# Spatial gating's columns in a two-layer hybrid backbone: features as the stationary operand, then a turn by chunk

## The chip, the cores and the metric

One core of one Trainium2 chip runs the whole program. The metric is device microseconds for one execution, taken as the median of several runs.

## The reference

Two layers over 512 latent tokens and 256 context tokens, 1024 features each. A layer is a half-step SwiGLU network, a token mixing, and another half-step SwiGLU network, each ahead of a normalisation that two conditions modulate. The token mixing projects its normalised input h once:

```
px = hx @ w_in[l]                     # 1024 -> 512 q, 512 k, 512 v, 512 u, 512 vs, 2048 gates
o_a = neighbourhood_attention(q, k, v, ...)
o_b = chunk_spatial_gating(gelu(u), gelu(vs), ln_g, ln_b, w_s, b_s)

def chunk_spatial_gating(u, v, ln_g, ln_b, w_s, b_s):
    vn = layernorm(v, ln_g, ln_b)     # over the 512 features of a token
    s = einsum('gpq,bnqgc->bnpgc', w_s, vn as chunks of 128 tokens, 4 groups of 128 features) + b_s
    return u * s
```

The context passes through the whole mixing in layer 0; in layer 1, the last, it only gives keys and values. Everything is float32 in and out.

## The kernel before

Features lie on partitions, tokens along the free axis. h is 16 tiles of 128 features by 768 tokens (512 latent, then 256 context): eight hold the high part and eight the low part of a float32 number split in two (hh, hl). A weight unit is 128 x 1024 numbers (512 KB); SyncE loads it (line 233), ScalarE writes its high part (line 222) and GpSimd the low part (line 223). A product is then three matmuls: high by high, high by low, low by high.

There are two forms of product. In `block` (line 327, with `mm3`, line 315) the weights are stationary, 128 columns of them, and h moves: 512 latent columns and, in layer 0, 256 context columns. The result has features on partitions. In `by_token` (line 942) 128 tokens of h are stationary and 256 columns of weights move, so that the result has tokens on partitions. `values` (line 954) uses it, as the attention needs its values by token, and so does `vs_half` (line 1184), since the layer norm of the gating reduces over features and its mixing over the 128 tokens of a chunk.

The latent tokens are ordered by grid column with the eight rows innermost. A gating chunk of 128 tokens is therefore every fourth latent column: `tokens(n)` (line 1179) gives `t[:, n:NX:4]` for the four latent chunks, and 128 neighbouring columns for the two of the context, which only layer 0 has (`n_ch` is 6 in layer 0 and 4 in layer 1). `vs_half(half)` makes 256 of the 512 features for all chunks, two chunks to a PSUM bank, and ScalarE copies each bank into tiles `vs` (line 1198).

The order of work on every engine is the order in which the program emits it. A list of tasks is run one after the other (`run`, line 300); each yields now and then, and at each yield `step` (line 288) runs one piece of the head of each of three lists, `side2` (rotary embedding) first, then `side` (attention, and behind it `gating`), then `side3`. So a piece of attention (scores, weighted sum, transposes of the shares, in `attention`, line 1096) stands between pieces of the products on TensorE. `by_token` is emitted whole, one yield a chunk; `block` yields every `EVERY[l]` row blocks (2 in layer 0, 3 in layer 1), and its callers once more at the end. PSUM has eight banks, from one list; the tiles of 128 x 768 come from one list of 38 (`t3`).

The tasks of a mixing run in this order: k and q of heads 0 to 3, `values(0)`, q and k of heads 4 to 7, `vs_half(0)`, `values(1)`, four `u_block` (line 1164: a `block` whose banks ScalarE copies into a tile, line 1172), `vs_half(1)`, then `gating` is put behind the attention, then sixteen blocks of gates (line 1285), and the merge. `gating` (line 1229) takes the gelu of the vs tiles (line 1236), normalises them by chunk and multiplies by the chunk's mixing weights; GpSimd multiplies the result into u (line 1227), again with a step of four for latent chunks.

Of the kernel before, what the change touches and what calls it, by code (L numbers as in the profile page):

```python
# [13 lines left out]
P = 128  # L14
# [52 lines left out]
# ---------------------------------------------------------------- host layout  # L67
# [27 lines left out]
def bias_layout(rpb):  # L95
    """Per head and kind of query tile, rpb laid out over (query, key); masked keys hold MASKED."""
# [17 lines left out]
def cols_units(w, order=None):  # L114
    """[K, N] -> [N/128, 128, (K/128) * 128]: one unit for each block of 128 columns."""
    k, n = w.shape
    return w.reshape(k // P, P, n // P, P).transpose(2, 1, 0, 3).reshape(n // P, P, k)


def close_units(w):  # L120
    """[K, 1024] -> [K/128, 128, 1024]: blocks of 128 by 128, all rows of the first columns first, eight to a unit."""
    n = w.shape[0] // P
    return w.reshape(n, P, KD, P).transpose(2, 0, 1, 3).reshape(n, KD, P, P).transpose(0, 2, 1, 3).reshape(n, P, D)


def half_units(w):
    """[1024, 512] -> [2 column halves, 2 k halves, 128, 4 * 256]."""
    return w.reshape(2, 4, P, 2, 256).transpose(3, 0, 2, 1, 4).reshape(4, P, 1024)


def layout(inp):
# [9 lines left out]
    # for each 128 columns of both of the first two: [128, 8 chunks of rows, 2 * 128 columns]  # L141
# [9 lines left out]
    for l in range(DEPTH):  # L151
        for n in ("1", "2"):
# [9 lines left out]
            q, k, half_units(w[:, 1024:1536]), cols_units(w[:, 1536:2048]), half_units(w[:, 2048:2560]),  # L162
# [26 lines left out]
# ---------------------------------------------------------------- weights  # L189
# [8 lines left out]
class Stream:  # L198
    """Loads weight units ahead of their use and splits each into two float32r parts."""

    def __init__(self, nc, pool, units, n_raw, n_hi):
        self.nc, self.pool, self.units = nc, pool, units
        # one slot spare: a load does not wait for the readers emitted last
# [4 lines left out]
    def advance(self, most=1):  # L208
        """Emit loads while there is room, and the splits of at most so many units."""
# [46 lines left out]
# ---------------------------------------------------------------- device  # L256
class Core:
# [12 lines left out]
    # ---- tiles  # L270
# [9 lines left out]
    # ---- scheduling of the emission  # L280
    def task(self, units, gen, own=False):
        """own: the task itself takes and drops its units."""
# [32 lines left out]
    # ---- products  # L315
    def mm3(self, out, groups, w, xs, first, last):
        """out[g] += w.T @ x over one block of 128 rows, in three float32r products."""
# [9 lines left out]
    def block(self, out, groups, unit, ks, xs, every=4):  # L327
        """One 128-column block: ks = columns of the unit for each k, xs = (hi, lo) for each k."""
# [7 lines left out]
    # ---- setup  # L336
    def setup(self):
# [12 lines left out]
        # brings in the table of the first norm's root ahead of it  # L350
        nc.scalar.activation(out=self.sm(16, "nw")[:, :1], in_=self.ones[:, :1], func=AF.Sqrt)
        # the two conditions sixteen times over, for each k
# [24 lines left out]
    # ---- tables of the token mixing and, in their place, the conditions for the modulation  # L377
# [20 lines left out]
    # ---- modulation  # L398
    def ada_units(self, l, idx):
        """Steps of one unit each, which together make mods[l][:, idx]."""  # L400
# [3 lines left out]
        def part(d, unit):  # L404
            """128 columns of the modulation, on partitions: sums over the rows for both conditions."""
# [34 lines left out]
    def extras(self, n):  # L440
        """On average n of the modulations' steps."""
# [6 lines left out]
    def require(self, l, idx):  # L448
        """The modulations up to this one, whatever of them is left."""
# [13 lines left out]
    # ---- norms  # L463
# [14 lines left out]
    def rowsum(self, box, grp):  # L478
        """Tiles of squares summed over partitions, four side by side, each on 32 partitions."""
# [11 lines left out]
    def rstd(self, box, grp, waits=(1, 1, 1), keep=False):  # L491
        """1 / sqrt(mean + eps) of the squares, on every partition (in PSUM, or in SBUF)."""
# [36 lines left out]
    def norm(self, l, i, box, h, grp, waits=(1, 1, 1), keep=False):  # L529
        """h[:, grp] = rmsnorm(x) * g * (1 + scale) + shift, in two float32r parts."""  # L530
# [31 lines left out]
    def split(self, name, src, grps):  # L562
        """(hi, lo) of a float32 tile or of its column groups."""
# [10 lines left out]
    # ---- accumulate into the residual stream  # L574
# [7 lines left out]
    def close(self, l, idx, units, xs, groups, box, after):  # L582
        """The last rows of a product into the stream, group after group; the norm of the first group
        runs beside the products of the second."""
        ks = len(xs)

        def gen():
            left = list(units)
            # brings in the table of the norm's root ahead of it
# [25 lines left out]
    # ---- first products of a phase, group after group  # L615
    def opening(self, blocks, groups, h, done):
        """Blocks of one unit each, the norm of each group (one of two in the background) just ahead of
        its products; done gets the PSUM tiles of each block."""
        def gen():
            out = [{} for _ in blocks]  # L620
            left = list(blocks)
            for gi, grp in enumerate(groups):
                self.drain_to(1 - gi)
                for o in out:
                    # two halves share their bank
# [21 lines left out]
    # ---- FFN  # L647
    def ffn(self, l, f, groups, hbox, xgroups, box, after, start=False):
# [38 lines left out]
        def begin():  # L687
            """The first modulation by columns, so that the products begin with its first columns."""
# [4 lines left out]
            def load(d):  # L693
                """Columns of the first two modulations, three chunks of rows to a tile."""
# [122 lines left out]
    # ---- the end  # L817
    def finish(self, groups, box):
        """The last norm; the products of the first of two groups fill the waits of the second."""
# [4 lines left out]
        def slot(d, grp):  # L824
            """Where the chunk goes: up to three chunks leave together."""
# [45 lines left out]
    # ---- token mixing  # L871
    def mixing(self, l, hbox, hgroups, xgroups, box, after):
# [14 lines left out]
        # q and k: rotary embedding on (even, odd) tiles of four heads  # L887
# [54 lines left out]
        def by_token(us, c, ps, at):  # L942
            """ps[:, at:at + 256] = h[:, tokens].T @ w, c = columns of h for the tokens."""
# [10 lines left out]
        def values(g):  # L954
            us = [unit(8 + 2 * g + s) for s in range(2)]

            def gen():
                # for each chunk and head (hi, lo) of 64 columns, six pairs to a tile
# [17 lines left out]
        # attention  # L976
# [12 lines left out]
        def stacks(raw):  # L989
            """One step for q, one for k."""  # L990
# [439 lines left out]
```

## Time and profile before

| | |
|---|---|
| median of three runs | 3034.73 us (3034.19 to 3035.49) |
| profiled execution, span from first to last instruction | 3031.9 us |
| between that span and the median | 2.8 us |
| TensorE busy in the span | 2998.1 us |
| VectorE, ScalarE, GpSimd busy | 1324.4, 906.4, 1138.1 us |
| mean DMA rate | 103 GB/s |

The page gives no total of its own for the profiled execution, so its time is its span and the 2.8 us that the median has beyond it. In the rows below, PE is TensorE's matmuls and PEld its weight loads, which overlap them; DVE is VectorE, ACT is ScalarE, POOL is GpSimd, SP is SyncE. "L950" is line 950 of the kernel. Names such as `ps<-whi,hh` give what is written and what is read. Matmuls are pipelined: a piece's length on the chain, or the distance from one start to the next, is what it costs the engine, while a matmul's own duration includes its way through the array. The chain of work that ended last is followed back from the last instruction; its pieces in order of time give the start, the length and the number of instructions.

### The profile page before, as it was taken

To read this page: it belongs to the slowest core of one execution; us is meant where nothing else is said; L and a number is where in the kernel's file an instruction comes from. 1 tells how busy PE (TensorE), PEld (TensorE's weight loads), DVE (VectorE), ACT (ScalarE), POOL (GpSimd) and SP (SyncE) were. 2 spreads that over 40 slices of the span, in tenths; PEclk is the share of its full clock that TensorE was granted. 3 is DMA by queue.
4 is the path that set the end of the run, shared out by engine and by line. 5 is a ranking of instruction groups with operands and counts; after the bars stand their busy time and mean duration, and the time that the engine had idled before them with its cause. 6 is when DMAs were issued, how large, how long until landed. Compare 5 with 4: busy or idle time off the path is not lost.

```text
span 3031.9 us, 41959 instructions
## 1 busy us (share of the span) xinstructions
PE 2998.1 (99%) x17036; PEld 2614.0 (86%) x17036; DVE 1324.4 (44%) x2256; ACT 906.4 (30%) x1493; POOL 1138.1 (38%) x708
## 2 busy tenths in 40 slices
PE   8999999999999999999999999999999999999998
PEld 5888888899998888888888888888888998888887
DVE  4554445536642444434445544544344643421113
ACT  4212112334652233111122411121233553332222
POOL 1323333444434243223233333332335545544443
PEclk9999999999999999999999999999999999999999
DMA  6333333333311132323333133332224322323222
GB/s 232 124 115 116 116 114 112 104 126 89 89 53 63 51 124 86 109 85 111 105 106 107 68 111 110 118 105 104 81 81 153 102 80 88 121 75 102 96 103 70
DMA packets 99888, 311.20 MB, mean 103 GB/s; under 512 B 12656, under 2 KB 14960, under 8 KB 99696
## 3 DMA queue, kind: packets, MB, share of 16 engines
q1 hardware_dynamic: 96704, 296.79, 29.2%
q0 software_dynamic: 2560, 11.54, 1.0%
q8 instruction: 134, 2.20, 0.3%
q14 instruction: 58, 0.48, 0.0%
q10 hardware_dynamic: 432, 0.20, 0.0%
HBM read 288.56 MB, written 8.39 MB: 98 GB/s over the span
## 4 chain that ended last, share of the span: by engine, by line
PE 95%; DVE 3%; DMA 1%; ACT 1%; issue 0%; POOL 0%; SPq 0%; ACTq 0%; DVEq 0%; POOLq 0%
PE ps L322 28%; PE ps L325 28%; PE ps L323 28%; PE ps L950 6%; PE ov L1073 1%; PE pt L1051 1%; DVE hl L550 1%; DVE nu L541 1%; PE sc L1016 0%; PE sc L1018 0%; DVE x L577 0%; PE ss L485 0%; DVE gt L1223 0%; DMA wraw<-up 0%; PE rs L519 0%
## 5 line engine op out<-in xcount | busy, mean ns | idle before, releaser
L223 POOL TENSOR_TENSOR wlo<-wraw,whi 128x1024 fp32r<-128x1024 f32 (+2 forms) x426 | 936.9, 2201 | 1606.1 <-ACT whi L222 1581.9
L322 PE MATMUL ps<-hh,whi 128*128 128x512 f32 (+1 forms) x3200 | 1115.1, 348 | 5.3 <-ACT hh L545 5.3
L323 PE MATMUL ps<-hl,whi 128*128 128x512 f32 (+1 forms) x3200 | 1049.0, 345 | 0.6 <-DVE hl L550 0.6
L325 PE MATMUL ps<-hh,wlo 128*128 128x512 f32 (+1 forms) x3200 | 906.5, 346 | 0.2 <-POOL wlo L223 0.2
L322 PEld LDWEIGHTS ps<-hh,whi 128*128 128x128 f32 x3200 | 602.2, 188 | 143.0 <-ACT hh L545 6.5
L222 ACT CAST whi<-wraw 128x1024 fp32r<-128x1024 f32 (+2 forms) x426 | 395.6, 931 | 997.4 <-PE ps L323 404.2
L323 PEld LDWEIGHTS ps<-hl,whi 128*128 128x128 f32 x3200 | 602.5, 188 | 78.9 <-DVE hl L550 1.9
L325 PEld LDWEIGHTS ps<-hh,wlo 128*128 128x128 f32 x3200 | 520.1, 190 | 24.5 <-POOL wlo L223 0.6
L322 PE MATMUL ps<-gh,whi 128*128 128x512 f32 (+1 forms) x1256 | 431.6, 344 | 0.0
L660 DVE TENSOR_TENSOR s<-s,ps 128x512 f32<-128x512 f32 (+1 forms) x154 | 82.3, 570 | 763.4 <-PE ps L325 710.8
L323 PE MATMUL ps<-gl,whi 128*128 128x512 f32 (+1 forms) x1256 | 407.9, 341 | 0.0
L577 DVE SCALAR_TENSOR_TENSOR x<-ps,mods,x 128x512 f32<-128x512 f32 (+1 forms) x344 | 203.2, 616 | 378.5 <-PE ps L325 378.2
L325 PE MATMUL ps<-gh,wlo 128*128 128x512 f32 (+1 forms) x1256 | 355.3, 342 | 0.0
L322 PEld LDWEIGHTS ps<-gh,whi 128*128 128x128 f32 x1256 | 236.2, 188 | 51.2 <-issue 1.6
L323 PEld LDWEIGHTS ps<-gl,whi 128*128 128x128 f32 x1256 | 236.3, 188 | 28.4
L409 DVE CUSTOM_DVE_ANT_0 wraw<-wraw,large 128x1024 f32<-128x1024 f32 x128 | 232.2, 1814 | 12.9 <-issue 0.5
L409 DVE CUSTOM_DVE_ANT_0 large<-wraw,large 128x1024 f32<-128x1024 f32 x128 | 220.4, 1722 | 0.0
L325 PEld LDWEIGHTS ps<-gh,wlo 128*128 128x128 f32 x1256 | 205.9, 190 | 8.9
L568 ACT CAST gh<-s 128x768 fp32r<-128x768 f32 (+1 forms) x88 | 68.7, 781 | 446.6 <-DVE s L660 446.6
L950 PE MATMUL ps<-whi,hh 128*128 128x256 f32 x352 | 117.3, 333 | 0.0
L950 PE MATMUL ps<-wlo,hh 128*128 128x256 f32 x352 | 114.0, 324 | 0.0
L950 PE MATMUL ps<-whi,hl 128*128 128x256 f32 x352 | 114.0, 324 | 0.0
(161 smaller groups left out, 2658.8 us busy)
## 6 DMA issues: line engine op xcount, KB each, us to landing
wraw<-up SPq DMA_DIRECT2D x176, 512.0 KB, 3.3
wraw<-ada SPq DMA_DIRECT2D x128, 512.0 KB, 3.3
wraw<-win SPq DMA_DIRECT2D x72, 512.0 KB, 3.3
wraw<-dm SPq DMA_DIRECT2D x96, 320.0 KB, 2.9
wraw<-dm SPq DMA_DIRECT2D x32, 256.0 KB, 2.6
wraw<-pab SPq DMA_DIRECT2D x16, 512.0 KB, 3.2
ch<-first SPq DMA_DIRECT2D x16, 384.0 KB, 7.4
wraw<-dl SPq DMA_DIRECT2D x12, 512.0 KB, 3.4
```

What stands on the lines that cost most here:

```text
L222: nc.scalar.copy(out=u.hi[:, :u.n], in_=u.raw[:, :u.n])
L223: nc.gpsimd.tensor_tensor(out=u.lo[:, :u.n], in0=u.raw[:, :u.n], in1=u.hi[:, :u.n].bitcast(F32), op=ALU.subtract)
L322: nc.tensor.matmul(out[g][:, :n], lhsT=wh, rhs=xh[:, o:o + n], start=first, stop=False)
L323: nc.tensor.matmul(out[g][:, :n], lhsT=wh, rhs=xl[:, o:o + n], start=False, stop=False)
L325: nc.tensor.matmul(out[g][:, :n], lhsT=wl, rhs=xh[:, o:o + n], start=False, stop=last)
L409: nc.vector.tensor_tensor_reduce(out=out, in0=unit.raw, in1=self.condb[c], scale=1.0, scalar=0.0, op0=ALU.mult, op1=ALU.add, accum_out=m[: ...
L541: nc.vector.scalar_tensor_tensor(out=us[d], in0=self.x[d][:, o:o + n], scalar=self.mod(l, 3 * i + 1, d, grp), in1=r, op0=ALU.mult, op1=ALU ...
L550: nc.vector.scalar_tensor_tensor(out=hl[e][:, o:o + n], in0=us[e], scalar=self.mod(l, 3 * i, e, grp), in1=hh[e][:, o:o + n].bitcast(F32), ...
L568: nc.scalar.copy(out=hi[:, o:o + n], in_=src[:, o:o + n])
L577: self.nc.vector.scalar_tensor_tensor(out=self.x[d][:, o:o + n], in0=ps[:, :n], scalar=self.mod(l, idx, d, grp), in1=self.x[d][:, o:o + n] ...
L660: nc.vector.tensor_tensor(out=s[:, o:o + n], in0=s[:, o:o + n], in1=out[1][gi][:, :n], op=ALU.mult)
L950: nc.tensor.matmul(ps[:, at:at + 256], lhsT=c(t[k]), rhs=w, start=k == 0 and i == 0, stop=k == KD - 1 and i == 2)
```

## The change

`vs_half` computes its columns with `block`, as `u_block` does: each of its two units gives 128 features on partitions for all tokens. ScalarE copies the banks into a tile `vt`, reading the latent columns with a step of four, so that the tile has them chunk after chunk. When both units of a half are there, a generator `turned` is put on `side2`: for each pair of chunks it transposes four blocks of 128 x 128 on TensorE into one PSUM bank, and ScalarE copies the bank into the vs tiles as before. `gating` yields until both halves are there. The host lays these weights out by blocks of 128 columns instead of by halves. Removed comments are not shown.

```
-            q, k, half_units(w[:, 1024:1536]), cols_units(w[:, 1536:2048]), half_units(w[:, 2048:2560]),
+            q, k, half_units(w[:, 1024:1536]), cols_units(w[:, 1536:2560]),
             cols_units(w[:, 2560:]),
...
         def vs_half(half):
-            us = [unit(16 + 2 * half + s) for s in range(2)]
-
-            def gen():
-                tiles = st["vs"][half] = [self.t3("vs") for _ in range(wide // 384 + (wide % 384 > 0))]
-                for n in range(0, n_ch, 2):
-                    ps = self.ps()
-                    for i in range(2):
-                        by_token(us, tokens(n + i), ps, 256 * i)
-                        yield
-                    for i in range(2) if n % 3 == 2 else (0,):
-                        w = 256 if n % 3 == 2 else 512
-                        c = n + i
-                        nc.scalar.copy(
-                            out=tiles[c // 3][:, (c % 3) * 256:(c % 3) * 256 + w], in_=ps[:, 256 * i:256 * i + w]
+
+            rows = []
+
+            def gen(un):
+                ps = [self.ps() for _ in qgroups]
+                yield from self.block(ps, qgroups, un, ks, list(zip(*h())), EVERY[l])
+                t = self.t3("vt")
+
+                nc.scalar.copy(
+                    out=t[:, :NX].rearrange("p (n i) -> p n i", n=4), in_=ps[0].rearrange("p (i n) -> p n i", n=4)
+                )
+                if len(ps) > 1:
+                    nc.scalar.copy(out=t[:, NX:], in_=ps[1][:, :NC])
+                rows.append(t)
+                if len(rows) == 2:
+                    self.side2.append(turned(half, rows))
+                yield
+
+            for s in range(2):
+                un = unit(16 + 2 * half + s)
+                self.task([un], lambda un=un: gen(un))
+
+        def turned(half, rows):
+            tiles = [self.t3("vs") for _ in range(wide // 384 + (wide % 384 > 0))]
+            for n in range(0, n_ch, 2):
+                ps = self.ps("vp")
+                for i in range(2):
+                    for s, t in enumerate(rows):
+                        nc.tensor.transpose(
+                            ps[:, 256 * i + P * s:256 * i + P * s + P], t[:, (n + i) * P:(n + i + 1) * P], self.eye
                         )
 
-            self.task(us, gen)
+                for i in range(2) if n % 3 == 2 else (0,):
+                    w = 256 if n % 3 == 2 else 512
+                    c = n + i
+                    nc.scalar.copy(
+                        out=tiles[c // 3][:, (c % 3) * 256:(c % 3) * 256 + w], in_=ps[:, 256 * i:256 * i + w]
+                    )
+                yield
+            rows.clear()
+            st["vs"][half] = tiles
...
+            while len(st["vs"]) < 2:
+                yield
             bs = self.t3("bs")[:, :512]
```

## Rows read from the trace of the kernel before

**Rows 1.** The page: TensorE busy, granted clock by slice, chain by engine, by line.
```profile
PE 2998.1 (99%) x17036; PEld 2614.0 (86%) x17036; DVE 1324.4 (44%) x2256; ACT 906.4 (30%) x1493; POOL 1138.1 (38%) x708
...
PEclk9999999999999999999999999999999999999999
...
PE 95%; DVE 3%; DMA 1%; ACT 1%; issue 0%; POOL 0%; SPq 0%; ACTq 0%; DVEq 0%; POOLq 0%
PE ps L322 28%; PE ps L325 28%; PE ps L323 28%; PE ps L950 6%; PE ov L1073 1%; PE pt L1051 1%; DVE hl L550 1%; DVE nu L541 1%; PE sc L1016 0%; PE sc L1018 0%; DVE x L577 0%; PE ss L485 0%; DVE gt L1223 0%; DMA wraw<-up 0%; PE rs L519 0%
```

**Rows 2.** TensorE's list of waits: us in total, times, longest us.
```profile
PE ss L485 <- ACT sq L469: 16.0, 7, 6.5
```

**Rows 3.** The chain in order of time, `vs_half`: start us, us, what.
```profile
700.11 5.61 PE ps L950 x24
...
720.43 5.61 PE ps L950 x24
...
727.19 2.87 PE ps L950 x24
...
731.22 2.88 PE ps L950 x24
...
734.81 0.44 PE pt L1051 x4
...
843.60 2.88 PE ps L950 x24
...
2345.61 5.61 PE ps L950 x24
...
2458.45 5.61 PE ps L950 x24
```

**Rows 4.** Weight loads in order of time, a latent and a context chunk: start us, us.
```profile
718.72 0.33 PEld L950 LDWEIGHTS ps<-whi,hl 128*128 128x128 f32 x1
...
727.03 0.19 PEld L950 LDWEIGHTS ps<-wlo,hh 128*128 128x128 f32 x1
```

**Rows 5.** The chain in order of time, first products of row blocks, layers 0 and 1.
```profile
654.49 0.23 PE ps L322
...
655.54 0.23 PE ps L322
...
2411.83 0.23 PE ps L322
...
2413.22 0.23 PE ps L322
```

**Rows 6.** Stretches with `u_block`: us, busy PE, PEld, DVE, ACT, POOL, clock, DMA, GB/s.
```profile
740.00:811.00 71.00, 71.00 (x513) 66.88 (x512) 50.16 (x134) 47.47 (x110) 38.40 (x38) 1.00 0.36 107
2403.00:2437.00 34.00, 34.00 (x214) 30.44 (x213) 26.33 (x63) 27.84 (x57) 25.51 (x23) 1.00 0.42 132
```

**Rows 7.** ScalarE's groups by shape: busy us, mean ns, idle before.
```profile
L1172 ACT COPY u<-ps 128x512 f32<-128x512 f32 x8 | 4.7, 584 | 4.5 <-POOL kb L999 3.7 <-PE ps L325 0.7
L1172 ACT COPY u<-ps 128x256 f32<-128x256 f32 x4 | 1.5, 379 | 0.0
```

**Rows 8.** GpSimd in order of time: latent chunk, context chunk, two multiplications each.
```profile
903.22 1.04 POOL L1227 TENSOR_TENSOR u<-u,gt 128x128 f32<-128x128 f32 x2 [3.31 <-DVE gt L1223]
...
925.97 0.92 POOL L1227 TENSOR_TENSOR u<-u,gt 128x128 f32<-128x128 f32 x2 [1.35 <-DVE gt L1223]
```

**Rows 9.** TensorE and ScalarE in order of time, at two ends of `u_block`.
```profile
772.03 0.28 PE L1016 MATMUL sc<-ka,qs 128*128 128x256 f32 x1
772.11 0.86 ACT L1172 COPY u<-ps 128x512 f32<-128x512 f32 x2
...
798.11 0.28 PE L1025 MATMUL sc<-ka,qs 128*128 128x256 f32 x1
800.28 0.86 ACT L1172 COPY u<-ps 128x512 f32<-128x512 f32 x2 [2.00 <-POOL kb L999]
```

**Rows 10.** Instructions on the vs tiles: ns min/median/max, first and last start.
```profile
L1236 ACT ACTIVATE vs<-vs x8: 401/831/847, 872.0 to 2483.1; 128x768 f32<-128x768 f32 x6, 128x256 f32<-128x256 f32 x2
```

## What I expect, before the run

> **What bounds the kernel now.** I read the page from the top. The first section has TensorE busy for 2998.1 of 3031.9 us, and the second shows nines in nearly every slice, with the granted clock at nine tenths or more throughout [rows 1]; so every us that leaves TensorE's stream leaves the run, unless TensorE then waits. The chain of work that ended last says the same: 95% of it is TensorE, and 6% of the whole is line 950, the helper `by_token` [rows 1]. It serves `values` and `vs_half`, and the change touches `vs_half` alone. The list of waits says how little is idle: its first line, a norm's, has the longest single wait of the run, 6.5 us, and lies far from the change [rows 2].
>
> Then the chain in order of time, for the first `vs_half` of layer 0 [rows 3]. Each piece "L950 x24" is one chunk of 128 tokens: 8 blocks of rows times three products. The reader is to see that the first four chunks take 5.61 us and the last two 2.87 and 2.88, with the same two weight units, the same columns (256) and the same attention work in between. The second half in layer 0 shows the same sequence, and layer 1, where `vs_half` has the four latent chunks only, shows 5.61 in all eight, of which the first and the last stand here [rows 3]. What sets the six chunks apart is `tokens(n)`: latent chunks take every fourth column of h (`t[:, n:NX:4]`) as the stationary operand, context chunks take 128 neighbouring ones. The weight loads show where the time is: 0.33 us with the strided columns, 0.19 with neighbouring ones; the spacing is set by them and no longer by the 256 moving columns [rows 4]. So 5.61 / 24 = 0.234 us a product instead of 0.120.
>
> **The products.** Removed, layer 0: two halves of four strided and two contiguous chunks, 8 x 5.61 + 4 x 2.87 = 56.4 us; layer 1: 8 x 5.61 = 44.9 us. Sum 101.2.
>
> Added: four blocks per layer of the kind that `u_block` has, with weights stationary and h moving, all contiguous. A row block of layer 0 (three products of 512 columns and three of 256) takes 1.05 us, from 654.49 to 655.54, and so on for those that follow [rows 5]: 4 x 8 x 1.05 = 33.6 us. In layer 1 it is three products of 512 columns; two row blocks run from 2411.83 to 2413.22, 0.695 us each [rows 5]: 4 x 8 x 0.695 = 22.2 us. Sum 55.8. The products save 101.2 - 55.8 = 45.4 us.
>
> The loads are as they were: 512 KB a unit, four per layer, on the same queue in the same place. They are now taken and given back one at a time, which frees a slot sooner; no cost. Where layer 1 already runs blocks at the new pace (2403 to 2437 us), DMA is busy for 0.42 of the time and TensorE never idles [rows 6].
>
> **The turn.** Added on TensorE: 24 transposes in layer 0 and 16 in layer 1, in ten groups of four. The attention's `turn` is the same instruction on the same shape, and a group of four takes 0.44 us on the chain [rows 3], refill included: 4.4 us, all on the path.
>
> Added on ScalarE: eight copies of 128x512 (four of them followed by 128x256), 0.59 and 0.38 us in the shape that `u_block` copies [rows 7]. That is 8 x 0.59 + 4 x 0.38 = 6.2 us in all, spread over stretches in which ScalarE is busy for 27.8 of 34 us at most [rows 6]. The copies out of the turned bank are as many and as large as those of line 1198 before.
>
> But the new copies read PSUM with a step of four elements, which no ScalarE row of this trace does. From below the price is nothing: 0.59 us. From above it is a doubling of the time per element, as in the strided weight load. The nearest rows: GpSimd multiplies two blocks of 128x128 in 1.04 us with a step of four and in 0.92 without [rows 8], a seventh more at a slow pace; the weight load doubles at a pace (0.12 us for 128 columns) close to ScalarE's own ((0.584 - 0.379) / 256 = 0.80 ns an element [rows 7]). I take the latter, for its pace: 512 more times 0.80 ns, so 1.0 us a copy, and keep 0.59 for the low end. [...]
>
> **The wait that is new.** `turned` goes into `side2` right after the copy of the second unit and `step` serves `side2` first. So the first transposes stand behind the block's last product on TensorE, and need a copy that can only begin when that product is done. TensorE is in order: the attention's scores, its weighted sums and the next block stand behind them. This happens once per half, four times in all; the later groups find their columns ready. The wait is ScalarE's lag, plus the copy, plus a hand-off. The lag I read from the eight copies of `u_block`, which stand in the same place. The block's end is the start of the next attention product; the copy starts between 0.08 us (772.03 to 772.11) and 2.17 us (798.11 to 800.28, waiting for GpSimd to give a tile back) later; all eight are at 0.08, 0.16, 2.17, 0.08, 0.12, 1.55, 0.20 and 0.25 us, mean 0.58 [rows 9]. The hand-off I put at 0.1 us, an estimate from the smallest lag. So 0.58 + 1.0 + 0.1 = 1.7 us, four times: 6.8 us. Low end 4 x (0.08 + 0.59 + 0.1) = 3.1; high end 4 x (2.17 + 1.0 + 0.1) = 13.1, and 0.8 more if the transposes of layer 0 wait for the context columns too.
>
> **What is moved.** A block yields more often than `by_token` did: 16 times against 12 in layer 0, 12 against 8 in layer 1. So the attention's steps are emitted up to four steps earlier, as many as before; TensorE's work for them is the same. They now come every 3.3 us or so (in layer 0 two row blocks, 2.1 us, and some 1.2 of attention) instead of every 6.8 ((720.43 - 700.11) / 3 [rows 3]); in the `u_block` stretches they already do, and TensorE is busy for all of 740 to 811 and 2403 to 2437 us, with ScalarE at 67% and 82% [rows 6]. I cost this at nothing; layer 1 has the thinner cover, and if it is gone, it shows as waits on ScalarE of the size of the lag. `gating` now waits until both halves are turned, but it stands behind the attention in the same list: its gelu begins at 872.0 us in layer 0 [rows 10], while the last half ended at 843.60 + 2.88 = 846.5 [rows 3]. No cost.
>
> **Sum.** -45.4 + 4.4 + 6.8 = -34.2 us. The profiled execution has a span of 3031.9 us, the median of the runs is 3034.73; the 2.8 us outside are not touched. 3034.7 - 34.2 = 3000.5 us. With the ends of the wait alone: 3034.7 - 45.4 + 4.4 + 3.1 = 2996.8 and 3034.7 - 45.4 + 4.4 + 13.9 = 3007.6.
>
> **Rivals.**
> First, slower than before: it isn't the step of four that doubles the chunk, and the latent columns are slow in any form (by where they lie in h, say). Its place is the latent chunks; its price is that their surplus of 16 x (5.61 - 2.87) = 43.8 us comes back in the new blocks. The products would then save 45.4 - 43.8 = 1.6 us against 4.4 + 6.8 = 11.2 of cost: 3034.7 + 9.6 = 3044.3. It decides once more than 34.2 of the 43.8 us come back. For it: place and step differ together in the rows. Against it: in every block the same latent columns stream as moving operand, 512 in 0.23 us, in step with the context's [rows 5]. The Trainium skill, page "TensorE: Matmul & The Clock Gate", section "LDWEIGHTS (loading the stationary operand)", counts a load by its columns alone and has no term for their step; by that this rival holds. The loads of one stretch, 0.33 and 0.19 us at the same 128 columns, contradict it [rows 4].
>
> Second, smaller gain: all ten groups wait, not four, because the copies out of the turned banks or the new tiles queue behind ScalarE's and GpSimd's attention work. The price is at most the high end for each group, 10 x 3.3 = 33 us: 3034.7 - 45.4 + 4.4 + 33 = 3026.7; half of them, 3010. For it: two of eight copies of `u_block` were 1.5 to 2.2 us late [rows 9], and ScalarE is at 82% in layer 1 [rows 6]. Against it: in those stretches TensorE didn't wait for any of it.
>
> **How the numbers follow.** Forecast 0.87 (its own range 2996.8 to 3007.6), first rival 0.02, second 0.10, and 0.01 for what I don't see. Predicted 3000.5 us. The range goes from 2993, a little under the low end for a transpose that is cheaper behind a wait, to 3013, where half of the second rival lies. About 0.2% (6 us) is what a measurement here can tell from no change: faster 0.96, same 0.02, slower 0.02.
>
> **What would show it.** In the trace of after: pieces of line 950 only from `values`, all near 2.87 us; the new blocks at 1.05 and 0.70 us a row block; ten groups of four transposes of 0.44 us; four idle spells of TensorE, of 0.8 to 3.3 us, each ended by the new copy on ScalarE; that copy's duration, 0.6 or 1.0 us; weight loads of 0.33 us gone. Wrong would be: loads still at 0.33 us, idle spells of TensorE at more than four places, or attention steps that leave TensorE idle between 2400 and 2470 us.

## The result, and the profile after

The median of four runs is 3005.1 us (3003.4 to 3007.5) against 3034.7 before: 29.6 us less, ratio 0.9904, 95% interval 0.9890 to 0.9918. The forecast was 3000.5, within 2993 to 3013; it was right in sign and 4.6 us too low. The profiled execution of after is the longest of its four: 3007.46 us, with a span of 3005.7 against 3031.9, so 26.2 us shorter. The points below are settled on this pair of spans.

The page of after, busy time by engine; the line of before is in [rows 1]:

```profile
PE 2964.6 (99%) x16884; PEld 2569.8 (85%) x16884; DVE 1324.8 (44%) x2256; ACT 912.6 (30%) x1505; POOL 1140.0 (38%) x708
```

TensorE still sets the time: its busy time fell by 33.5 us, the span by 26.2. The 7 us between the two are idle time that was not there before.

TensorE in order of time (start us, us, what; in brackets idle time before it and what ended it). First the new row blocks in layer 0 and in layer 1, then the first transposes behind a block in both layers, then the gating's products of two chunks:

```profile
704.94 0.39 PE L322 MATMUL ps<-hh,whi 128*128 128x512 f32 x1
...
705.99 0.28 PE L1016 MATMUL sc<-ka,qs 128*128 128x256 f32 x1
...
2334.11 0.39 PE L322 MATMUL ps<-hh,whi 128*128 128x512 f32 x1
...
2334.79 0.39 PE L322 MATMUL ps<-hh,whi 128*128 128x512 f32 x1
...
726.27 0.55 PE L1213 MATMUL vp<-eye,vt 128*128 128x128 f32 x3 [0.45 <-ACT vt L1193]
...
736.03 0.60 PE L1213 MATMUL vp<-eye,vt 128*128 128x128 f32 x4
736.38 0.37 PE L1016 MATMUL sc<-ka,qs 128*128 128x256 f32 x1
736.59 0.28 PE L1016 MATMUL sc<-kb,qs 128*128 128x256 f32 x1
...
2354.19 0.90 PE L1213 MATMUL vp<-eye,vt 128*128 128x128 f32 x3 [2.56 <-ACT vt L1193]
...
897.47 0.28 PE L1234 MATMUL sg<-wsx,vnh 128*128 128x256 f32 x1
...
903.62 0.58 PE L1234 MATMUL sg<-wsx,vnh 128*128 128x256 f32 x1 [2.88 <-ACT vnh L568]
```

A row block takes 705.99 - 704.94 = 1.05 us in layer 0 and 2334.79 - 2334.11 = 0.68 in layer 1, as in the `u_block` of before [rows 5]. A group of four transposes that waits for nothing takes 0.35 us up to the next product, and that one's successor comes 0.09 late (0.21 apart, not 0.12): 0.44 in all. Line 950 is left with the products of `values`.

TensorE's waits that are new or have grown (us in total, times, longest us):

```profile
PE vp L1213 <- ACT vt L1193: 4.0, 4, 2.6
PE sg L1234 <- ACT vnh L568: 3.6, 2, 2.9
PE sg L1234 <- DVE vnl L569: 0.6, 2, 0.4
```

The first line is the wait that the forecast has. The second is one that it costed at nothing: the gating's products for the last chunk of layer 0 stand 2.88 us. (Its other entry, 0.8 us in layer 1, is 0.6 in before.)

The new copy of line 1193 by its tile (ns, shortest/median/longest):

```profile
L1193 ACT COPY vt<-ps x8: 573/587/587, 712.6 to 2436.7; 128x512 f32<-128x512 f32 x8
```

It reads PSUM with a step of four elements and takes 0.587 us, no more than the contiguous copy of [rows 7], 0.584.

Windows on TensorE around the two longest of these waits, and at a norm further on (us, busy PE, granted clock, DMA share, GB/s):

```profile
900.00:904.00 4.00, 1.12 (x6) 0.89 0.37 131
904.00:908.00 4.00, 3.79 (x15) 0.50 0.00 0
908.00:912.00 4.00, 4.00 (x19) 0.76 0.01 4
...
2352.00:2356.00 4.00, 1.81 (x9) 0.72 0.74 191
2356.00:2360.00 4.00, 4.00 (x26) 0.85 0.40 124
...
2629.00:2636.00 7.00, 6.04 (x35) 0.76 0.22 75
```

The granted clock falls to 0.50, the 1.2 GHz level, and comes back. In 904 to 908 TensorE is busy again, at half speed: the products of 256 columns there take 0.41 us instead of 0.28. In the profile of before the clock is at half once behind the start of the run and not again before its end; after has 6.8 us of it in layer 0, 3.4 us in layer 1 and 3.4 us in the norm at 2630.

To see what each stage gives I took the start of the last product of each task on TensorE in each trace, and the distances between these; the first row of a layer begins with the first product of `values(0)`, and the first `vs_half` ends with the first product of the `values(1)` behind it. The table has the lengths in before, and for the other kernels the difference from it (us, worked out from the traces). Attention steps move from one stage to another, so single rows mix tasks; the sum of a layer doesn't.

```
stage                    before  after  again   late    gap   both noturn  twice shift1 shift2
L0 attention: q1, k1      61.61   0.03   0.05   0.05   0.04   0.06   0.05   0.04   0.07   0.04
   first vs_half          36.87  -7.95  -7.94  -9.04  -7.94  -9.07  -9.03  -7.50  -7.94  -7.95
   values                 23.31   0.86   0.86   1.29   0.86   1.28   0.01   1.77   0.86   0.86
   u_block                52.20  -1.15  -1.15  -1.15  -1.15  -1.15  -1.16  -1.15  -1.15  -1.15
   second vs_half         35.14  -9.06  -9.06  -9.06  -9.06  -9.06  -9.05  -9.06  -9.06  -9.06
   gates, with gating    147.24   4.61   3.66   3.84  -1.70  -2.36   1.61   3.36  -1.74  -0.53
   sum of layer 0           -   -12.66 -13.58 -14.07 -18.95 -20.30 -17.57 -12.54 -18.96 -17.79
L1 attention: q1, k1      51.60  -0.04  -0.03  -0.04  -0.06  -0.04  -0.01  -0.03  -0.05  -0.06
   first vs_half          29.95  -4.08  -4.04  -8.64  -5.41  -8.64  -8.54  -4.99  -5.42  -4.26
   values                 24.50  -2.37  -2.34  -0.35  -2.36  -0.32  -0.44  -1.91  -2.36  -1.87
   u_block                37.27   0.09   0.00   0.09   0.09   0.00   0.04   0.00   0.09   0.09
   second vs_half         28.01  -9.04  -9.04  -9.04  -9.04  -9.04  -9.04  -9.04  -9.04  -9.04
   gates, with gating     96.79  -0.33  -0.30  -1.10  -2.01  -2.79  -1.96   0.59  -0.68  -0.68
   sum of layer 1           -   -15.77 -15.75 -19.08 -18.79 -20.83 -19.95 -15.38 -17.46 -15.82
projection to next norm  119.12   1.51   1.51   1.50   0.02   1.35   1.37   0.01   1.34   0.03
```

The stages left out agree within 0.4 us, but for the start of the run (0.3 to 2.7 us longer than in this run of before, all of it within the first 50 us) and, in `late` alone, a feed-forward stage with a fall of its own (3.1 us).

The books of the pair: the products -45.4, the transposes +4.5, the waits behind the blocks +4.7, the new part of the gating's waits +4.1, the clock +5.0 (2.2 in layer 0, 1.3 in layer 1, 1.5 in the norm), the start of the run +0.7. That is -26.4, and the spans differ by -26.2. The 4.7 are more than the 4.0 of the list, which counts idle time alone: from the first transpose to the product behind the group it is 1.03, 1.03 and 1.14 us at the three short waits instead of 0.35, so 0.7, 0.7 and 0.8 us, and 2.6 at the long one. At the start after has 10.2 us at half clock and before 6.8, but runs with 6.8 are longer there by up to 1.8 us too, so that this piece isn't shown to be the clock's. How the others were taken apart follows.

### The profile page after: what moved, and what is told of

It is laid out like the page before. It is cut to its first block, busy times and chain, and to the rows that moved or that the text cites. A ratio compares the mean times of both kernels' runs of the same rounds, so it can differ in the third digit from the quotient of the medians.

```text
span 3005.7 us, 41669 instructions
## 1 busy us (share of the span) xinstructions
PE 2964.6 (99%) x16884; PEld 2569.8 (85%) x16884; DVE 1324.8 (44%) x2256; ACT 912.6 (30%) x1505; POOL 1140.0 (38%) x708
## 4 chain that ended last, share of the span: by engine, by line
PE 67%; DVE 2%; ACT 1%; issue 1%; POOL 0%; DMA 0%; SPq 0%; DVEq 0%; ACTq 0%; POOLq 0%
PE ps L322 21%; PE ps L325 21%; PE ps L323 21%; PE ps L950 1%; DVE hl L550 1%; PE ov L1073 0%; PE pt L1051 0%; DVE gt L1246 0%; DVE x L577 0%; DVE nu L541 0%; PE ss L485 0%; PE sc L1016 0%; PE sc L1018 0%; DVE vn L1297 0%; PE rs L519 0%
## 5 line engine op out<-in xcount | busy, mean ns | idle before, releaser
L322 PE MATMUL ps<-hh,whi 128*128 128x512 f32 (+1 forms) x3296 | 1152.6, 350 | 5.3 <-ACT hh L545 5.3
L323 PE MATMUL ps<-hl,whi 128*128 128x512 f32 (+1 forms) x3296 | 1083.2, 346 | 0.6 <-DVE hl L550 0.6
L325 PE MATMUL ps<-hh,wlo 128*128 128x512 f32 (+1 forms) x3296 | 936.9, 346 | 0.2 <-POOL wlo L223 0.2
L322 PEld LDWEIGHTS ps<-hh,whi 128*128 128x128 f32 x3296 | 621.4, 189 | 146.6 <-ACT hh L545 6.6
L323 PEld LDWEIGHTS ps<-hl,whi 128*128 128x128 f32 x3296 | 621.8, 189 | 81.3 <-DVE hl L550 1.9
L325 PEld LDWEIGHTS ps<-hh,wlo 128*128 128x128 f32 x3296 | 537.3, 190 | 26.0 <-POOL wlo L223 0.6
L569 DVE TENSOR_TENSOR gl<-s,gh 128x768 fp32r<-128x768 f32 (+1 forms) x88 | 79.4, 902 | 74.6 <-ACT gh L568 74.6
L659 ACT ACTIVATE s<-ps 128x512 f32<-128x512 f32 (+1 forms) x154 | 70.2, 500 | 43.9 <-PE ps L325 43.9
L469 ACT ACTIVATE sq<-x 128x256 f32<-128x256 f32 (+1 forms) x104 | 51.7, 499 | 96.7 <-DVE x L577 95.0
```

Of the source, the lines that this page charges most:

```text
L322: nc.tensor.matmul(out[g][:, :n], lhsT=wh, rhs=xh[:, o:o + n], start=first, stop=False)
L323: nc.tensor.matmul(out[g][:, :n], lhsT=wh, rhs=xl[:, o:o + n], start=False, stop=False)
L325: nc.tensor.matmul(out[g][:, :n], lhsT=wl, rhs=xh[:, o:o + n], start=False, stop=last)
L469: self.nc.scalar.activation(out=sq, in_=x, func=AF.Square)
L569: nc.vector.tensor_tensor(out=lo[:, o:o + n], in0=src[:, o:o + n], in1=hi[:, o:o + n].bitcast(F32), op=ALU.subtract)
L659: nc.scalar.activation(out=s[:, o:o + n], in_=out[0][gi][:, :n], func=AF.Silu)
```

## The experiments

Ten kernels are spoken of here: the two of the change and eight more. Where several runs are given, they were made on one chip beside runs of the kernel before; "after again" is the changed kernel in such a set.

### The changed kernel again

It has no edit.

> The changed kernel once more, beside the three that follow. Every theory: 3003 to 3008 us. If the granted clock's falls depend on where a wait happens to lie, the runs scatter by 1.2 to 3.5 us with the share of the clock; if nothing of the kind is at work, they agree within 1 us.

Measured: 3007.1 us (3006.1 to 3010.8), 28.6 under the kernel before of the same set (3035.75), ratio 0.9909 (0.9894 to 0.9923). The runs scatter by 4.7 us, more than was expected. All the waits are there again. The fall in layer 0 lasts 3.4 us instead of 6.8, and its stage is 0.95 us shorter (+3.66 against +4.61). Of the same program, the second profile thus already gives one price of the clock.

### The transposes one step later

```diff
         def turned(half, rows):
+            yield
             tiles = [self.t3("vs") for _ in range(wide // 384 + (wide % 384 > 0))]
```

> The turn begins one yield later: a first bare yield in `turned`, so that an attention step and the next row blocks stand between the copy and the first transposes. Theory A (the four waits for the copy, 4.7 us by the trace of after, and the 3.4 us at half clock that follow the longest of them, are on the path): TensorE's waits for vt are gone, 3005.1 - 4.7 - 1.5 = 2998.9 us, between 2997 and 3001. Rival B (the wait moves: with the turn later its copies or the gating are late instead, or TensorE waits for the same engines elsewhere): within 2 us of after.

Measured: 3004.9 us (3000.7 to 3006.4), 2.3 less than after again in the median, a gain smaller than the 4 to 8 us expected and within the scatter. Its list of waits has no entry for `vp`; instead:

```profile
PE pt L1051 <- DVE sp L1045: 1.4, 1, 1.4
PE sg L1235 <- ACT vnh L568: 3.6, 2, 2.9
```

So one step of attention or block is enough to cover ScalarE's copy. Layer 1, where the long wait was, gains 19.08 - 15.75 = 3.3 us, of which 1.3 is the fall of the clock that is missing, although the attention, no longer held up, now waits 1.4 us for VectorE. Layer 0 gains only 0.5: its two waits were short (the row of 0.45 us above is one), and the gating's wait stands, with a fall of 6.8 us where after again had 3.4. The profiled run of `late` also has a fall of 6.8 us at 2250 us in a feed-forward stage that no edit touches, worth 3.1 us. The wait is taken away as expected; how much of it the time shows depends on the clock.

### A gap before the last chunk of the gating

```diff
                 if held:
+                    if n == n_ch:
+                        yield
+                        yield
                     gate(n - 1, *held)
```

> Two more yields of `gating` ahead of its last chunk, so that four more row blocks stand between the next to last chunk's products and the last one's. Theory A (the 2.9 us that the last chunk's products wait in layer 0, and the 6.8 us at half clock behind it, are lost on the path; the chain through VectorE is merely short of cover there): the wait is gone and no fall of the clock stands there, 3005.1 - 3.1 - 3.1 = 2998.9, between 2997 and 3001. Rival B (the wait is noise that other runs of after don't have, or it moves to the next step): within 2 us of after.

Measured: 2999.5 us (2997.4 to 3001.5), 7.6 less than after again; ratio to before 0.9884 (0.9867 to 0.9900). The waits on `vnh` and `vnl` are gone in both layers, the falls in layers 0 and 1 and in the norm too. The window over the place in layer 0, here with all engines (busy PE, PEld, DVE, ACT, POOL, clock, DMA, GB/s), first in `gap`:

```profile
876.00:912.00 36.00, 36.00 (x223) 32.19 (x222) 27.61 (x52) 15.78 (x31) 18.57 (x25) 1.00 0.13 45
```

and in after:

```profile
876.00:912.00 36.00, 32.91 (x186) 29.01 (x185) 25.32 (x52) 13.63 (x27) 19.05 (x27) 0.91 0.11 41
```

TensorE issues 223 products instead of 186 in the same 36 us. Layer 0 gains 5.4 us on after again, layer 1 gains 3.0 (1.7 of it in the gating: the last chunk's wait, which before has too; 1.3 where the fall at 2353 is missing), the norm 1.5 (and the start of this run is 1.1 longer). This wait, at a place that the forecast calls free, is the largest of the terms that it lacks.

### Both edits

The diff is that of the two before, together.

> Both edits. Theory A, if the two losses are independent: 3005.1 - 6.2 - 6.2 = 2992.7 us, between 2990 and 2996; that is 3034.7 - 45.4 + 4.4, with nothing lost on waits (2993.7). Rival B: one of them gives nothing, 2998 to 3001; or neither, 3003 to 3006.

Measured: 2995.8 us (2994.9 to 2997.0), ratio to before 0.9869 (0.9855 to 0.9884): 40.0 us less than before and 11.4 less than after again, at the upper end of what was expected. Of the new waits one is left:

```profile
PE pt L1051 <- DVE sp L1045: 1.4, 1, 1.4
```

This version beats both kernels. It also gives the sum of products and transposes almost alone. Layer 0 is at -20.30; the forecast's terms are 33.6 - 56.4 = -22.8 for the products and 6 x 0.45 = 2.7 for the transposes, so -20.1. Layer 1: 22.2 - 44.9 + 4 x 0.45 = -20.9; measured -20.83, in which the new 1.4 us and the last chunk's wait of before (0.6 and 0.4 us, now gone) about cancel. The -45.4 us stand within some 0.5.

### Columns at steps of 1 to 6

On the kernel before: the latent chunks' stationary columns at other distances, with the step of context chunks left as it is.

```diff
+        def spaced(n):
+            s = ((1, 2, 3, 4), (5, 6, 2, 1))[l][n] if n < 4 else 0
+            return (lambda t: t[:, 0:P * s:s]) if s else tokens(n)
...
-                        by_token(us, tokens(n + i), ps, 256 * i)
+                        by_token(us, spaced(n + i), ps, 256 * i)
```

> The kernel before, in which a latent chunk of `vs_half` takes 128 columns of h with another step than four: in layer 0 the four chunks take steps 1, 2, 3, 4 from the first column, in layer 1 steps 5, 6, 2, 1 (so other tokens than the reference's; nothing is left out). Theory A (the step makes the weight load slow, by how many elements of one 16-byte piece a load uses): 2.87 us a chunk at steps 1 and 2, 5.61 at 4, 5 and 6, something between at 3. Rival B (the place does it: latent columns are slow at any step): 5.61 at all eight. Rival C (the load is slow as the bytes that it passes over): 2.87 at 1, then rising with every step, 5.61 at 4 and above that at 5 and 6.

The chain of `steps` in order of time, one line for each chunk: layer 0 with steps 1, 2, 3, 4, then layer 1 with 5, 6, 2, 1 (before: [rows 3]):

```profile
701.10 2.86 PE ps L950 x24
...
705.12 2.88 PE ps L950 x24
...
709.17 4.17 PE ps L950 x24
...
714.51 5.61 PE ps L950 x24
...
2332.79 5.49 PE ps L950 x24
...
2339.66 5.49 PE ps L950 x24
...
2346.54 2.88 PE ps L950 x24
...
2350.81 2.88 PE ps L950 x24
```

Its weight loads, at steps 1, 3 and 4:

```profile
701.40 0.19 PEld L950 LDWEIGHTS ps<-whi,hl 128*128 128x128 f32 x1
...
709.75 0.26 PEld L950 LDWEIGHTS ps<-whi,hl 128*128 128x128 f32 x1
...
715.39 0.33 PEld L950 LDWEIGHTS ps<-whi,hl 128*128 128x128 f32 x1
```

A step of 2 is free, 3 costs half of it, 4 the whole, and 5 and 6 no more than 4. That is the picture of pieces of 16 bytes, four float32, which are read at full pace as long as two columns fall into each: with a step of 3 that is so for two columns in every four, from 4 on for none. The chunk at step 3, 4.17 us, lies near the middle of 2.87 and 5.61, as this asks. The Trainium skill, page "SBUF — State Buffer", in its note on SBUF cachelines, says that consecutive accesses to one line of 16 bytes run at full bandwidth, with at least two hits in each line, and that a crossing to a new line costs. The rows agree for the weight load, but not with the note's figure for the step that is free, "4 fp32": here 2 is free, and 4 costs the whole. The whole time agrees: a half of layer 0 gains 2.75 + 2.73 + 1.44 = 6.9 us by these rows, one of layer 1 twice 0.12 and twice 2.73, so 5.7; two halves each make 25.2, and 3035.8 - 25.2 = 3010.6, with 3011.0 measured in one run. Nothing is turned here and nothing new waits, so the distance of the columns alone makes the gain.

So the first rival, latent columns that are slow wherever they stand, has fallen twice: here, and in the row blocks of after.

### No transposes

```diff
-                ps = self.ps("vp")
-                for i in range(2):
-                    for s, t in enumerate(rows):
-                        nc.tensor.transpose(
-                            ps[:, 256 * i + P * s:256 * i + P * s + P], t[:, (n + i) * P:(n + i + 1) * P], self.eye
-                        )
+                ps = rows[n // 2 % 2]
```

> The changed kernel without the transposes: ScalarE copies the tiles vt into the vs tiles as they stand, with the same number and sizes of copies; the turn is left out. What remains of the change on TensorE are the products. Theory A (products save 45.4 us, transposes cost 4.4, the waits for the copy and the half clock behind them 6.2): 3005.1 - 4.4 - 6.2 = 2994.5 us, 2992 to 2997, with the wait of the gating's last chunk still there. Rival B (the products save less than the strided rows say, and the turn is cheaper): 2998 or more.

Measured: 3000.2 us (2998.2 to 3001.0), ratio 0.9883 (0.9865 to 0.9901), 7 less than after again and some 6 more than expected. By the number alone, rival B holds: the products save less than the strided rows say. The list of waits and the stages say otherwise:

```profile
PE pt L1051 <- DVE sp L1045: 2.1, 1, 2.1
PE sg L1228 <- ACT vnh L568: 3.6, 2, 2.9
```

The gating's wait is untouched, it brought a fall of 3.4 us with it again, and the attention of layer 1, held up less, runs into a wait of 2.1 us for VectorE. Taken out, layer 0 is at -17.57 - 3.9 - 1.2 = -22.7 and layer 1 at -19.95 - 2.1 = -22.1, against -22.8 and -22.7 for the products without transposes. The expectation lacked what stays and what comes new.

### Every group of transposes twice

```diff
-                    for s, t in enumerate(rows):
+                    for s, t in list(enumerate(rows)) * 2:
```

> The changed kernel with every transpose of the turn emitted twice in a row, into the same place: ten groups of eight instead of four. Theory A (a transpose in a group costs its spacing, 0.09 us, and the refill behind a group comes once): 40 x 0.088 = 3.5 us more in the stages that turn, 0.35 for each group of the trace. Rival B (a group costs 0.44 us each time): 4.4 us. Rival C (transposes are hidden behind the waits): under 1 us.

In `twice`, one doubled group in order of time:

```profile
738.07 1.04 PE L1213 MATMUL vp<-eye,vt 128*128 128x128 f32 x8
738.86 0.37 PE L1016 MATMUL sc<-ka,qs 128*128 128x256 f32 x1
```

Eight take 0.79 us up to the next product where four took 0.35: 0.44 for the second four, as rival B has it; theory A's 0.35 is too low. The stages agree: the first `vs_half` of layer 0, with one extra group, is longer by 7.95 - 7.50 = 0.45, `values` with two by 0.91. The whole time was 3007.6 us in one run, about that of after again, although ten groups more are worth 4.5 us. Where that went is seen in windows of all engines (columns as under the gap) around the two long waits, which are there again with 2.9 and 2.6 us:

```profile
904.00:908.00 4.00, 0.89 (x5) 0.38 (x3) 3.21 (x8) 1.30 (x3) 2.11 (x4) 1.00 0.37 131
...
2352.00:2356.00 4.00, 1.44 (x10) 1.00 (x9) 3.54 (x7) 2.24 (x6) 3.76 (x4) 1.00 0.56 137
```

The clock stays at 1.00. The same waits with no fall behind them give the price of each separately. Gates of layer 0: 3.36 - 2 x 0.45 = +2.46 without a fall; +3.66 in after again with 3.4 us at half, +4.61 in after with 6.8: a fall costs 1.2 or 2.2 us there. And the wait itself: in `twice` its products start 3.1 us later than the spacing of the products before them gives, the second 0.7 and the third 0.1 later again, 3.9 us in all, of which the list of waits has 2.9 and 0.4.

### The gating shifted by one step, and by two

```diff
             while len(st["vs"]) < 2:
                 yield
+            for _ in range(1):     # range(2) in shift2
+                yield
             bs = self.t3("bs")[:, :512]
```

> The changed kernel with one bare yield at the start of `gating`, so that the gating begins one step later against the blocks of gates. In the order of ScalarE the gates' tanh (a load of its table and two activations, 2.3 us in the trace of after) then stands between the first and the second chunk's split, no longer right ahead of the copies of the first chunk's products. Theory A (where the gating falls against the gates decides: in after VectorE's chain starts 2.3 us late behind that tanh, never gains it back, and the last chunk's wait of 2.9 us is what is left of it): the wait in layer 0 changes by the order of 2 us, to under 1.2 us. Rival B (twelve products between the last two chunks are too few in any case, as in the kernel before they only just were enough): the wait stays between 2.4 and 3.4 us.

> The same with two bare yields: the tanh with its table then stands ahead of the first chunk's split, and the copies of the first products follow the splits at once. Theory A: VectorE's chain starts without the 2.3 us, and the last chunk's wait in layer 0 is under 1.2 us. Rival B: it stays between 2.4 and 3.4 us.

One run each: 2999.9 us with one step, 3003.1 with two, and 3034.65 for the kernel before on the same chip. With one step TensorE waits for nothing between 860 and 930 us, and the gates of layer 0 are at -1.74, as with the gap (-1.70). With two steps 0.4 and 0.3 us of waiting are left, and the stage is at -0.53. In layer 1 the last chunk goes on waiting, 1.3 us with one step and 1.0 with two (1.2 in after, 1.0 in before). So the 2.9 us are no property of the new operations: they depend on where the gating's steps fall among the gates' blocks, which the change moved because its blocks yield another number of times.

How far it moved them is seen at the last products of the attention in layer 0, in before and in after:

```profile
867.24 0.40 PE L1073 MATMUL ov<-ptt,v 128*128 128x256 f32 x2
...
842.90 0.40 PE L1073 MATMUL ov<-ptt,v 128*128 128x256 f32 x2
```

In before they stand at the seventh yield of the gates, in after at the fourth. The blocks of `vs_half` yield four times more, but one of these passes without the attention (no piece of it stands between the last chunk of `values(1)` and the first `u_block`, at 752.58 in after). A block of gates yields four times, so that three steps earlier is one place further on in a block. With one and two steps more, the runs have the gating at all four places: it waits in layer 0 for nothing in before, 2.9 and 0.2 us in after, nothing in `shift1`, 0.7 us in `shift2`.

What the place in the block, the phase, does is to be read on ScalarE, after the products of the gating's first chunk. In after:

```profile
876.83 0.28 PE L1234 MATMUL sg<-wsx,vnh 128*128 128x256 f32 x1
877.01 0.62 ACT L568 CAST vnh<-vn 128x512 fp32r<-128x512 f32 x1 [1.41 <-DVE vn L1297]
877.65 1.28 ACT L1325 ACT_TABLE_LOAD   x1
878.94 1.05 ACT L1325 ACTIVATE ga<-ps,half_gate 128x512 f32<-128x512 f32 x2
879.88 0.65 ACT L1241 COPY gt<-sg 128x256 f32<-128x256 f32 x2
```

and in `shift1`:

```profile
876.08 1.28 ACT L1327 ACT_TABLE_LOAD   x1
877.37 1.05 ACT L1327 ACTIVATE ga<-ps,half_gate 128x512 f32<-128x512 f32 x2
878.31 0.62 ACT L568 CAST vnh<-vn 128x512 fp32r<-128x512 f32 x1
880.47 0.65 ACT L1241 COPY gt<-sg 128x256 f32<-128x256 f32 x2 [1.54 <-PE sg L1234]
```

In after, the table load and the gates' tanh stand between the chunk's products (they start at 876.83) and the copies of `gt` that follow from them: 3.05 us. In `shift1` ScalarE is through with both and waits for the products. In before the copy comes 0.68 us after them (901.17 to 901.85). Behind the copy is VectorE's chain, which normalises the next chunks; it ends late at the last one:

```profile
898.41 2.19 DVE L1246 SCALAR_TENSOR_TENSOR gt<-gt,cols,off 128x128 f32<-128x128 f32 x2
...
901.78 1.13 DVE L1297 TENSOR_SCALAR vn<-vs,lw 128x256 f32<-128x256 f32 x2
```

`vn` of the last chunk begins at 901.78, when TensorE already stands, and between the last two chunks there are only 12 products of a block to cover it (24 between the others). That the phase decides is shown by the two shifts, and that more cover does away with the wait too, by the gap. That the table load is the piece of it that counts is read from these lines and wasn't tried alone; the first of VectorE's two lines, 2.19 us beside a GpSimd split at 897.78 where the same pair takes 0.61 at 893.03, is a second piece that I did not separate.

## Why the prediction was right, and where it was off

**The bound and the products: right.** TensorE set the time and the weight load set its pace in the latent chunks. The new row blocks came out at 1.05 and 0.68 us (0.695 was read), and the layers' sums in `both` confirm -45.4 within 0.5 us. `steps` shows why: the distance of the columns, not their place.

**The transposes: right.** 0.44 to 0.45 us a group, by `twice` and by the row of after; 4.5 us against 4.4.

**The wait behind the blocks: right in place and number, too high in size.** Four waits and no more, each ended by the new copy, as forecast; the second rival, with all ten groups waiting, did not come true. In size it was 4.7 us instead of 6.8. The term at fault is the copy: I took the upper bound of 1.0 us from the strided weight load, and it was 0.587, the lower one. That takes 1.6 us off the sum; the lags are the rest. The Trainium skill's page "Advanced Engine Details and Errata", section "PSUM Cachelines", says that a non-contiguous access to PSUM slows matmuls significantly; of a copy on ScalarE it says nothing, and to that the step of four elements cost nothing here. The lags were three short ones and one of the long kind that [rows 9] show: the copy in layer 1 started at 2353.56, behind a copy that had waited 1.14 us for GpSimd:

```profile
2351.97 0.37 ACT L1082 COPY ot<-ov 64x256 f32<-64x256 f32 x1 [1.14 <-POOL oa L1092]
...
2353.56 0.57 ACT L1193 COPY vt<-ps 128x512 f32<-128x512 f32 x1
```

**"What is moved ... No cost": wrong, 4.1 us (3.9 in layer 0, 0.2 in layer 1).** This is the step that failed. The argument compared the end of the last half with the start of the gating's gelu, and found room. That room was real, but the question was another one: a task that yields another number of times shifts every later task against the blocks it shares the engines with. The gating's last chunk had the thinnest cover, 12 products, already in before: there layer 1 waited 0.6 and 0.4 us. I had looked for the cover of the attention only. The forecast's own sign of being wrong, idle spells of TensorE at more than four places, is met by it: the 2.88 us at 903.62 are a fifth.

**The clock: not in the sum, 5.0 us in the profiled run.** "The granted clock at nine tenths or more throughout" was taken for granted of the new stream too. Two of the falls stand right behind the two longest waits that the change brought. But the clock's share differs between executions: `twice` had the same waits of 2.9 and 2.6 us and no fall, after again a shorter one in layer 0. The wait of 2.6 us in layer 1 stands in six profiles; a fall follows in after, after again and `shift2`, and none in `gap`, `twice` and `shift1`. Over all runs the lower clock does come with the waits: its mean is 0.997 or 0.998 in the fourteen runs of before beside the experiments and 0.997 in all four of `both`, but 0.995 or 0.996 in seven of the eight of the changed kernel. The four runs of after lie in the order of their mean granted clock, from 3003.4 us at 0.997 to 3007.5 at 0.995. A fall in the norm behind layer 1 (2630 us in after) is in six of the nine profiles with the change, not in those of `gap`, `twice` and `shift2`, and in that of `steps`, which has not the change; what brings it I can't say.

**The sum.** Off by +4.1 (gating) + 5.0 (clock) + 0.7 (start) - 2.1 (waits) + 0.1 (transposes) = 7.8 us for the profiled run, from -34.2 to -26.4. By the median the miss is 4.6, since that run is 2.3 us above its median, and since the 2.8 us that I added outside the span were too many: for after they are 3007.46 - 3005.7 = 1.8, so the profiled execution of before probably was about 1 us under its own median. The upper end of the range had room for both, put there for another reason (longer waits behind the blocks), so that the range held is luck in part.

**What stayed open.** Why the same wait is followed by a fall in one run and by none in the next; the falls in the norm and that of `late` at 2250 us; and how the 2.9 us of the gating's wait divide between ScalarE's table load and VectorE's stretched pair.

## What to carry to other kernels

When a matmul's operand has to be read in steps, read the spacing of its products against that of a contiguous one: a factor of two in it may be worth a different order of operands, even at the price of transposes. A change in the number of steps that a task takes moves every later task that is interleaved with it, so look at the places with the thinnest cover, the last piece of a chain above all, and not only at the place of the edit. And a wait of TensorE may cost more than its length; give it a term for the clock, and take a few runs before its size is believed.

## What was not expected of the hardware

A strided weight load costs by pieces of 16 bytes, not in proportion to the step: 128 columns of float32 take 0.19 us at steps of 1 and 2, 0.26 at 3, 0.33 at 4 and 0.32 at 5 and 6. A copy on ScalarE that reads PSUM at a step of four float32 runs at the pace of a contiguous one (0.587 us and 0.584 for 128x512). A stand of 2.6 to 2.9 us on TensorE was followed by 6.8, by 3.4 or by no us at the 1.2 GHz level, which cost 2.2, 1.2 to 1.3 or nothing beyond the wait.
